# The second feed-forward of an encoder layer by one level of Strassen's algorithm

## Chip, cores and metric

The kernel runs on one core of a Trainium2 chip. The metric is the device time of one execution in microseconds (us). The profile calls the engines PE (TensorE: matmuls; PEld is its weight load), DVE (VectorE), ACT (ScalarE), POOL (GpSimd) and SP (SyncE, which here only issues transfers).

## The reference

One encoder layer on 512 tokens of 1024 channels. Its last part, which the change touches, is a gated feed-forward with 2816 hidden units, behind a norm and a modulation:

```
x = x + g2[:, None, :] * y                       # y: output projection of the token mixing
h = modulate(rms_norm(x, ffn2_norm[l]), sh3, sc3)
x = x + 0.5 * g3[:, None, :] * (silu(h @ w_gate) * (h @ w_up)) @ w_down
return rms_norm(x, final_norm)
```

Before it stand a first feed-forward of the same size, a Fourier branch and an attention branch, and an output projection.

## The kernel before

Activations are held transposed: 128 channels on the partitions, tokens along the free dimension. All data is float32, and every matrix product is made of three: `split` and `split_to` turn a tile into `hi` (a rounded copy, made on ACT, L94 and L107) and `lo` (the residual, a subtraction on DVE, L95 and L108), and `mm3` (L101) runs hi x hi, hi x lo and lo x hi into the same PSUM bank.

The hidden units come in 22 chunks of 128. `ffn` (L244) goes over four parts of 6, 6, 6 and 4 chunks. For each chunk it fetches a unit of `wg` and one of `wu` (each 128 x 1024, 512 KB), splits both, and multiplies them by all 8 chunks of `h`: `products`, 24 matmuls of 512 columns each. `hidden` applies Silu to the gate, multiplies by the up-projection and splits the result. After each part the down projection adds its share to `x` for 8 output chunks. In the second feed-forward the first two chunks (L266 to L274) run in two halves of 256 tokens, so that TensorE can work on the first half while the second is still being normed. The last part's down projection runs in halves too, and `final` norms and stores each half.

Ahead of it, the output projection runs in two parts. The second part (L802 to L821) works by token halves: 8 output chunks into PSUM, added to `x` on DVE (L818), squared on ACT (L229), summed on DVE (L233); then `make_h` makes that half's `h`. In it `inv_rms` (L138) gets the inverse root from two tiny matmuls (L145), a scaling on DVE (L150), a power on POOL (L152), two diagonal tiles on DVE (L157) and a matmul that spreads them (L160). `scaled` (L187) multiplies on DVE into a `t` tile, of which there are two, and `shifted` makes hi on ACT (L194) and lo on DVE (L195).

Tiles come from pools: 5 `raw` tiles for fetched weights, 6 `hi` and 6 `lo` for split ones, 30 general slots of 128 x 1024 (`flex`, by `slot` and `slot32`), two each of the small kinds in `tmp`, 6 PSUM banks for products (`pbank`). A planner orders each engine's instructions when the program is built: it plays the program through with its own costs and gives a free engine the earliest instruction of the text that is ready. On the chip each engine then runs its list in order. Transfers issued by SP wait in SP's queue for a free tile.

## Time and profile before

| | us |
|---|---|
| median of three runs (lowest to highest) | 1095.09 (1093.96 to 1095.14) |
| the profiled execution | 1093.35 |
| its span | 1091.5 |
| TensorE busy in the span | 1067.0 |
| VectorE busy | 607.3 |
| ScalarE busy | 397.5 |

The span reaches from the first to the last instruction that the profiler recorded; the execution's own time is 1.85 us longer. An engine is busy while an instruction runs on it; instructions of one engine overlap a little at their ends, so the distance between starts tells its pace.

### The profile page before, as it was taken

To read this page: it belongs to the slowest core of one execution; us is meant where nothing else is said; L and a number is where in the kernel's file an instruction comes from. 1 tells how busy PE (TensorE), PEld (TensorE's weight loads), DVE (VectorE), ACT (ScalarE), POOL (GpSimd) and SP (SyncE) were. 2 spreads that over 40 slices of the span, in tenths; PEclk is the share of its full clock that TensorE was granted. 3 is DMA by queue.
4 is the path that set the end of the run, shared out by engine and by line. 5 is a ranking of instruction groups with operands and counts; after the bars stand their busy time and mean duration, and the time that the engine had idled before them with its cause. 6 is when DMAs were issued, how large, how long until landed. Compare 5 with 4: busy or idle time off the path is not lost.

```text
span 1091.5 us, 13823 instructions
## 1 busy us (share of the span) xinstructions
PE 1067.0 (98%) x5320; PEld 900.8 (83%) x5320; DVE 607.3 (56%) x1043; ACT 397.5 (36%) x631; POOL 87.0 (8%) x102
## 2 busy tenths in 40 slices
PE   5999999999999999999999989999999999999996
PEld 3888888888888998888888878998888888888886
DVE  6976645862563689752167767784343334334335
ACT  5532222222222444442267664353222222222224
POOL 1000000000000001000155444000000000000000
PEclk9999999999999999999999999999999999999998
DMA  9885642762472156541121223423242233224102
GB/s 360 329 317 166 226 149 87 234 211 76 147 237 99 58 202 218 176 143 39 39 64 54 59 95 108 154 78 107 89 134 82 73 116 116 73 82 135 59 1 78
DMA packets 48643, 143.76 MB, mean 132 GB/s; under 512 B 5489, under 2 KB 9201, under 8 KB 48578
## 3 DMA queue, kind: packets, MB, share of 16 engines
q1 hardware_dynamic: 46738, 137.84, 38.5%
q0 software_dynamic: 1264, 4.52, 1.1%
q8 instruction: 42, 0.69, 0.3%
q10 hardware_dynamic: 576, 0.52, 0.1%
q14 instruction: 23, 0.19, 0.1%
HBM read 138.67 MB, written 4.19 MB: 131 GB/s over the span
## 4 chain that ended last, share of the span: by engine, by line
PE 94%; DVE 2%; ACT 1%; issue 1%; DMA 1%; POOL 1%; SPq 0%; POOLq 0%; DVEq 0%; ACTq 0%
PE ps_mm L102 29%; PE ps_mm L104 29%; PE ps_mm L103 29%; PE ps_mm L324 3%; PE ps_mm L712 1%; PE ps_aux L704 1%; DMA g<-in_xtok 1%; PE ps_aux L160 1%; ACT f L107 0%; PE ps_aux L145 0%; ACT g L692 0%; PE ps_mm L528 0%; PE ps_aux L204 0%; POOL f L108 0%; DVE g L828 0%
## 5 line engine op out<-in xcount | busy, mean ns | idle before, releaser
L103 PE MATMUL ps_mm<-f,hi 128*128 128x512 f32 (+1 forms) x1504 | 550.6, 367 | 0.1
L102 PE MATMUL ps_mm<-f,hi 128*128 128x512 f32 (+1 forms) x1504 | 550.5, 367 | 0.0
L104 PE MATMUL ps_mm<-f,lo 128*128 128x512 f32 (+1 forms) x1504 | 550.1, 366 | 0.0
L94 ACT CAST hi<-raw 128x1024 fp32r<-128x1024 f32 (+4 forms) x207 | 188.3, 913 | 514.5 <-PE ps_mm L103 468.8
L104 PEld LDWEIGHTS ps_mm<-f,lo 128*128 128x128 f32 x1504 | 283.4, 189 | 45.9
L103 PEld LDWEIGHTS ps_mm<-f,hi 128*128 128x128 f32 x1504 | 283.4, 189 | 45.7 <-DVE f L195 0.3
L102 PEld LDWEIGHTS ps_mm<-f,hi 128*128 128x128 f32 x1504 | 283.0, 189 | 45.9 <-ACT f L107 0.6
L95 DVE TENSOR_TENSOR lo<-raw,hi 128x1024 fp32r<-128x1024 f32 (+3 forms) x195 | 213.2, 1095 | 175.5 <-ACT hi L94 171.9
L248 DVE TENSOR_TENSOR sg<-ps_mm,sg 128x512 f32<-128x512 f32 x44 | 30.3, 690 | 128.7 <-PE ps_mm L104 127.9
L133 DVE SCALAR_TENSOR_TENSOR raw<-raw,g 128x1024 f32<-128x1024 f32 x56 | 68.3, 1221 | 33.7 <-DMA raw<-in_ada_w 33.7
L290 DVE SCALAR_TENSOR_TENSOR g<-ps_mm,gate,g 128x512 f32<-128x512 f32 x48 | 35.9, 749 | 56.9 <-PE ps_mm L104 56.9
L152 POOL TENSOR_TENSOR r<-ms,nhalf 128x2 f32<-128x2 f32 x10 | 9.5, 958 | 663.4 <-DVE ms L150 663.4
L107 ACT CAST f<-sg 128x512 fp32r<-128x512 f32 x44 | 27.4, 623 | 18.8 <-DVE sg L248 18.7
L108 DVE TENSOR_TENSOR f<-sg,f 128x512 fp32r<-128x512 f32 x44 | 30.0, 684 | 0.7 <-ACT f L107 0.7
L247 ACT ACTIVATE sg<-ps_mm 128x512 f32<-128x512 f32 x44 | 25.9, 591 | 10.3 <-PE ps_mm L104 9.1
L692 ACT ACTIVATE g<-ps_mm,st 128x512 f32<-128x512 f32 x32 | 22.1, 691 | 19.5 <-DVE st L691 17.2
L324 PE MATMUL ps_mm<-f,hi 128*128 128x512 f32 x96 | 26.5, 414 | 0.7 <-ACT f L210 0.7
L694 POOL TENSOR_SCALAR g<-g,st 128x512 f32<-128x512 f32 x32 | 22.5, 704 | 38.5 <-DVE st L693 31.2
L229 ACT ACTIVATE sq<-g 128x256 f32<-128x256 f32 x42 | 17.0, 413 | 21.1 <-DVE g L308 13.6
L108 DVE TENSOR_TENSOR f<-ps_aux,f 128x512 fp32r<-128x512 f32 x32 | 21.7, 685 | 4.8 <-ACT f L107 4.7
L233 DVE TENSOR_TENSOR ssum<-ssum,sq 128x256 f32<-128x256 f32 x42 | 17.7, 422 | 11.6 <-ACT sq L229 11.4
L133 DVE SCALAR_TENSOR_TENSOR g<-g,g 128x1024 f32<-128x1024 f32 x16 | 19.5, 1219 | 6.8 <-ACT g L351 6.8
(152 smaller groups left out, 723.1 us busy)
## 6 DMA issues: line engine op xcount, KB each, us to landing
raw<-in_ada_w SPq DMA_DIRECT2D x56, 512.0 KB, 4.5
raw<-in_wu SPq DMA_DIRECT2D x45, 512.0 KB, 3.8
raw<-in_wg SPq DMA_DIRECT2D x41, 512.0 KB, 3.5
raw<-in_wd SPq DMA_DIRECT2D x48, 384.0 KB, 3.2
raw<-in_win SPq DMA_DIRECT2D x21, 512.0 KB, 3.5
g<-in_ada_w SPq DMA_DIRECT2D x16, 512.0 KB, 9.3
raw<-in_wd SPq DMA_DIRECT2D x16, 256.0 KB, 2.9
raw<-in_wout SPq DMA_DIRECT2D x16, 256.0 KB, 2.7
```

The costliest lines, as they stand in the source:

```text
L94: nc.scalar.copy(hi[:, :n], raw[:, :n])
L95: engine.tensor_sub(lo[:, :n], raw[:, :n], hi[:, :n].bitcast(F32))
L102: nc.tensor.matmul(out, lhsT=lh, rhs=rh, start=first, stop=False)
L103: nc.tensor.matmul(out, lhsT=lh, rhs=rl, start=False, stop=False)
L104: nc.tensor.matmul(out, lhsT=ll, rhs=rh, start=False, stop=last)
L107: nc.scalar.copy(hi, src)
L108: engine.tensor_sub(lo, src, hi.bitcast(F32))
L133: nc.vector.scalar_tensor_tensor(raw, raw, 1.0, cb.rearrange("p c t -> p (c t)"), op0=ALU.mult, op1=ALU.mult, accum_out=mod[:, j:j + 1])
L247: nc.scalar.activation(sg, pg, AF.Silu)
L248: nc.vector.tensor_mul(sg, pu, sg)
L290: nc.vector.scalar_tensor_tensor(xs(m), out, gate[gk][:, m:m + 1], xs(m), op0=ALU.mult, op1=ALU.add)
L324: nc.tensor.matmul(out[i], lhsT=w[:, i * P:(i + 1) * P], rhs=h1[c][:, part], start=c == 0 and w is wh and part == 0, stop=c == NC - 1 and ...
```

## The change

The gate and up projections of the second feed-forward take two chunks of hidden units at a time (a `Pair`), and multiply them by one level of Strassen's algorithm in Winograd's form. The 1024 x 256 weight matrix is four blocks of 512 x 128, and `h` four blocks of 512 channels x 256 tokens. Seven products of such blocks stand in place of eight, each 4 x 3 matmuls of 256 columns.

On the side of `h`, `make_blocks` makes seven split blocks in place of `h3`: "21" and "11" from the first token half, and from the second "22" and the combinations t1 to t4, each made in place by one operation on 128 x 1024 and then split. On the side of the weights, `_blocks` lays the four blocks out on the host; SP fetches two of them (`first`) and a third (`last`), and the two sums s1 and s3 are made by transfer: SP writes the fourth block twice (`broadcast_to`), and a transfer issued by POOL adds two others onto it (`accum_op`). DVE makes s2 and s4 from these. So a pair has seven splits of 128 x 1024 (`a1` two, `s31` two, `s24` two, `a22` one).

A pair is computed in two steps. `begin` needs only the first token half: two products per matrix into a bank `R1`, whose halves are added to give the first result's tokens. `rest` runs the other five: they accumulate into `R1` and a second bank `R2`, and partial sums are copied out by ACT between products onto the same half of a bank. A first product clears with `start`; the later ones add on (`onto`).

The transfers of the first two pairs (both `first` tiles, and for pair 0 the sums) are issued during the output projection, into general slots; the `begin` of both comes before the `rest` of the first. The down projection takes the last two chunks in reversed order, since a pair finishes its second chunk first.

```diff
-    def mm3(out, lh, ll, rh, rl, first, last):
-        nc.tensor.matmul(out, lhsT=lh, rhs=rh, start=first, stop=False)
-        nc.tensor.matmul(out, lhsT=lh, rhs=rl, start=False, stop=False)
-        nc.tensor.matmul(out, lhsT=ll, rhs=rh, start=False, stop=last)
+    def mm3(out, lh, ll, rh, rl, first, last, onto=False):
+        nc.tensor.matmul(out, lhsT=lh, rhs=rh, start=first, stop=False, skip_group_check=onto)
+        nc.tensor.matmul(out, lhsT=lh, rhs=rl, start=False, stop=False, skip_group_check=onto)
+        nc.tensor.matmul(out, lhsT=ll, rhs=rh, start=False, stop=last, skip_group_check=onto)
...
     def ffn(h, wg, wu, wd, gk, lead, background, after):
+        paired = wg.shape[0] != NF
...
-            elif pi == 0:
-                w = [unit(t[i], D) for i in range(2) for t in (wg, wu)]
-                out = [pbank() for _ in w]
-                for lo, hi in halves:
-                    for i in range(4):
-                        products(f + i // 2, w[i], out[i], lo, hi)
-                for i in range(2):
-                    act.append(hidden(*out[2 * i:2 * i + 2]))
-                f += 2
-            for f in range(f, f0 + nk):
+            elif paired:
+                for i in range(f0 // 2, (f0 + nk) // 2):
+                    pr = ahead[i] if i < len(ahead) else Pair((wg, wu), i)
+                    if i >= len(ahead):
+                        pr.first_weights()
+                    if i == 0:
+                        for p in ahead:
+                            p.first_weights()
+                            p.begin()
+                    pr.weights()
+                    if i >= len(ahead):
+                        pr.begin()
+                    act += pr.rest()
+            for f in range(f, f0 + nk if not paired else 0):
...
+            order = [*range(nk - 2), nk - 1, nk - 2] if paired else [*range(nk)]
...
-                    for k in range(nk):
+                    for k in order:
                         ks = slice(k * P, (k + 1) * P)
-                        mm3(out, dh[:, ks], dl[:, ks], act[k][:, 0], act[k][:, 1], k == 0, k == nk - 1)
+                        mm3(out, dh[:, ks], dl[:, ks], act[k][:, 0], act[k][:, 1], k == 0, k == order[-1])
...
+    class Block:
+        def __init__(self):
+            self.hi, self.lo = (flex.tile([P, 4, HALF], F32R, tag="f", name=nm("b")) for _ in range(2))
+    def make_blocks(lo, hi, ssq, key, sh, half, B, whole):
+        R = inv_rms(ssq.acc, D, hi - lo)
+        def combine(name, src):
+            B[name] = Block()
+            split_to(B[name].hi, B[name].lo, src)
+        def chunk(c):
+            t, _ = scaled(c, lo, hi, R, key)
+            nc.scalar.activation(whole[half][c // 4][:, c % 4], t, AF.Identity, bias=mod_of(sh, c))
+        if half == 0:
+            B["21"], B["11"] = Block(), Block()
+            for k, name in ((1, "21"), (0, "11")):
+                for c in range(4):
+                    chunk(4 * k + c)
+                    split_to(B[name].hi[:, c], B[name].lo[:, c], whole[0][k][:, c])
+            return
+        (h11, h21), (h12, h22) = whole
+        for c in range(4):
+            chunk(c)
+        nc.vector.tensor_sub(h11, h11, h12)
+        combine("t1", h11)
+        for c in range(4, NC):
+            chunk(c)
+        nc.vector.scalar_tensor_tensor(h11, h11, -1.0, h22, op0=ALU.mult, op1=ALU.subtract)
+        combine("t2", h11)
+        nc.vector.tensor_sub(h12, h22, h12)
+        combine("t3", h12)
+        nc.vector.scalar_tensor_tensor(h21, h11, -1.0, h21, op0=ALU.mult, op1=ALU.subtract)
+        combine("t4", h21)
+        combine("22", h22)
+    class Pair:
+        def __init__(self, ws, i, room=None, sums=False):
+            self.ws, self.i, self.sums = ws, i, None
+            room = room or (lambda: wpool.tile([P, SLOT], F32, tag="raw", name=nm("raw")))
+            if sums:
+                self.fetch_sums(room)
+            self.first = []
+            for w in ws:
+                raw = room()
+                nc.sync.dma_start(raw, w[i][:, 0::2])
+                self.first.append(raw)
+            self.E1, self.E2, self.R1, self.R2 = [], [], [], []
+        def fetch_sums(self, room):
+            self.sums = []
+            for w in self.ws:
+                raw = room()
+                nc.sync.dma_start(raw, w[self.i][:, 3:4].broadcast_to([P, 2, S]))
+                nc.gpsimd.dma_start(raw, w[self.i][:, 0:2], accum_op=ALU.add)
+                self.sums.append(raw)
+        def first_weights(self):
+            self.a1 = [split(r, D) for r in self.first]
+        def weights(self):
+            if self.sums is None:
+                self.fetch_sums(lambda: wpool.tile([P, SLOT], F32, tag="raw", name=nm("raw")))
+            last = wpool.tile([P, SLOT], F32, tag="raw", name=nm("raw"))
+            for j, w in enumerate(self.ws):
+                nc.sync.dma_start(last[:, j * S:(j + 1) * S], w[self.i][:, 1])
+            self.s31 = [split(r, D) for r in self.sums]
+            self.s24 = []
+            for r, t in zip(self.first, self.sums):
+                nc.vector.tensor_add(r[:, :S], t[:, S:], r[:, :S])
+                nc.vector.tensor_add(r[:, S:], r[:, :S], r[:, S:])
+                self.s24.append(split(r, D))
+            self.a22 = split(last, D)
+        def product(self, out, w, at, b, first):
+            for c in range(4):
+                cs = slice(at * S + c * P, at * S + (c + 1) * P)
+                mm3(out, w[0][:, cs], w[1][:, cs], h3[b].hi[:, c], h3[b].lo[:, c], first and c == 0, c == 3, not first)
+        def begin(self):
+            for u in range(2):
+                R1 = pbank()
+                self.R1.append(R1)
+                self.product(R1[:, :HALF], self.a1[u], 1, "21", True)
+                self.product(R1[:, HALF:], self.a1[u], 0, "11", True)
+                E1 = tmp.tile([P, S], F32, tag=("sg", "t")[u], name=nm("E1"))
+                self.E1.append(E1)
+                nc.scalar.copy(E1[:, :HALF], R1[:, HALF:])
+                nc.vector.tensor_add(E1[:, :HALF], R1[:, :HALF], E1[:, :HALF])
+            g, up = self.E1
+            nc.scalar.activation(g[:, :HALF], g[:, :HALF], AF.Silu)
+            nc.vector.tensor_mul(g[:, :HALF], up[:, :HALF], g[:, :HALF])
+        def rest(self):
+            for u in range(2):
+                R2 = pbank()
+                self.R2.append(R2)
+                self.product(R2[:, :HALF], self.s31[u], 1, "t1", True)
+                self.product(self.R1[u][:, HALF:], self.s24[u], 0, "t2", False)
+                nc.scalar.copy(self.E1[u][:, HALF:], self.R1[u][:, HALF:])
+            for u in range(2):
+                self.product(self.R1[u][:, HALF:], self.s31[u], 0, "t3", False)
+                E2 = tmp.tile([P, HALF], F32, tag=("sq", "ssum")[u], name=nm("E2"))
+                self.E2.append(E2)
+                nc.scalar.copy(E2, self.R1[u][:, HALF:])
+                nc.vector.tensor_add(E2, self.R2[u][:, :HALF], E2)
+            sg = slot32()[:, 0]
+            for u in range(2):
+                self.product(self.R1[u][:, HALF:], self.a22, u, "t4", False)
+            nc.scalar.activation(sg[:, HALF:], self.E2[0], AF.Silu, scale=-1.0)
+            nc.vector.scalar_tensor_tensor(sg[:, HALF:], self.E2[1], -1.0, sg[:, HALF:], op0=ALU.mult, op1=ALU.mult)
+            nc.scalar.activation(sg[:, :HALF], self.R1[0][:, HALF:], AF.Silu, scale=-1.0)
+            nc.vector.scalar_tensor_tensor(sg[:, :HALF], self.R1[1][:, HALF:], -1.0, sg[:, :HALF], op0=ALU.mult, op1=ALU.mult)
+            second = slot()
+            split_to(second[:, 0], second[:, 1], sg)
+            for u in range(2):
+                self.product(self.R2[u][:, :HALF], self.s24[u], 1, "22", False)
+                E1 = self.E1[u][:, HALF:]
+                nc.vector.tensor_add(E1, self.R2[u][:, :HALF], E1)
+                if u == 0:
+                    nc.scalar.activation(E1, E1, AF.Silu)
+            g, up = self.E1
+            nc.vector.tensor_mul(g[:, HALF:], up[:, HALF:], g[:, HALF:])
+            s = slot()
+            split_to(s[:, 0], s[:, 1], g)
+            return [s, second]
...
+    def room():
+        return slot32().rearrange("p h t -> p (h t)")
+    h3 = {}
+    ahead = [Pair((a["wg2"], a["wu2"]), i, room, not i) for i in range(2)]
     units = []
     for m in range(0, NC, 2):
         raw = wpool.tile([P, SLOT], F32, tag="raw", name=nm("raw"))
         for j in range(2):
             nc.sync.dma_start(raw[:, j * 4 * P:(j + 1) * 4 * P], a["wout"][m + j, :, 4:8, :])
         units.append(split(raw, SLOT))
-    h3 = [slot() for _ in range(NC)]
+    whole = [[flex.tile([P, 4, HALF], F32, tag="f", name=nm("w")) for _ in range(2)] for _ in range(2)]
...
-        make_h(h3, lo, hi, ssq, "3", SH3)
+        make_blocks(lo, hi, ssq, "3", SH3, lo // HALF, h3, whole)
...
-    ffn(h3, a["wg2"], a["wu2"], a["wd2"], "3", None, lambda: None, final)
+    ffn(None, a["wg2"], a["wu2"], a["wd2"], "3", None, lambda: None, final)
...
+def _blocks(w):
+    u = _units(w).reshape(NF // 2, 2, P, 2, S)
+    return np.ascontiguousarray(np.stack([u[:, 0, :, 0], u[:, 1, :, 1], u[:, 0, :, 1], u[:, 1, :, 0]], axis=2))
...
-        "wg2": _units(v["ffn2_w_gate"][0]), "wu2": _units(v["ffn2_w_up"][0]), "wd2": _units(v["ffn2_w_down"][0]),
+        "wg2": _blocks(v["ffn2_w_gate"][0]), "wu2": _blocks(v["ffn2_w_up"][0]), "wd2": _units(v["ffn2_w_down"][0]),
```

## Rows read from the trace of the kernel before

**Rows 1.** The page: busy time of the engines, and the chain that ended last, by engine.
```profile
PE 1067.0 (98%) x5320; PEld 900.8 (83%) x5320; DVE 607.3 (56%) x1043; ACT 397.5 (36%) x631; POOL 87.0 (8%) x102
...
PE 94%; DVE 2%; ACT 1%; issue 1%; DMA 1%; POOL 1%; SPq 0%; POOLq 0%; DVEq 0%; ACTq 0%
```

**Rows 2.** Windows at the hand-over: busy time by engine, clock, DMA share, GB/s.
```profile
684.00:707.00 23.00, 23.00 (x160) 21.26 (x158) 17.11 (x30) 7.63 (x14) 0.71 (x1) 1.00 0.48 159
707.00:719.00 12.00, 11.85 (x98) 11.79 (x98) 11.08 (x29) 9.34 (x18) 0.00 (x0) 1.00 0.00 1
719.00:731.00 12.00, 11.98 (x98) 11.66 (x97) 10.85 (x23) 3.15 (x7) 1.61 (x1) 1.00 0.51 177
731.00:742.50 11.50, 11.50 (x91) 11.16 (x90) 7.99 (x12) 8.31 (x11) 0.00 (x0) 1.00 0.33 89
```

**Rows 3.** Timeline of PE, matmuls of 512 and of 256 columns: start, duration.
```profile
684.98 0.39 PE L102 MATMUL ps_mm<-f,hi 128*128 128x512 f32 x1
...
691.55 0.39 PE L104 MATMUL ps_mm<-f,lo 128*128 128x512 f32 x1
691.77 0.28 PE L102 MATMUL ps_mm<-f,hi 128*128 128x256 f32 x1
...
694.89 0.28 PE L104 MATMUL ps_mm<-f,lo 128*128 128x256 f32 x1
```

**Rows 4.** Timeline of DVE, 719 to 726.
```profile
719.36 1.22 DVE L95 TENSOR_TENSOR lo<-raw,hi 128x1024 fp32r<-128x1024 f32 x1
720.50 0.42 DVE L233 TENSOR_TENSOR ssum<-ssum,sq 128x256 f32<-128x256 f32 x1
720.83 1.22 DVE L95 TENSOR_TENSOR lo<-raw,hi 128x1024 fp32r<-128x1024 f32 x1
...
725.38 0.86 DVE L189 SCALAR_TENSOR_TENSOR t<-g,G,ps_aux 128x256 f32<-128x256 f32 x2
```

**Rows 5.** Timeline of ACT: first and last of four casts, and three in succession.
```profile
706.94 1.05 ACT L94 CAST hi<-raw 128x1024 fp32r<-128x1024 f32 x1 [1.08 <-PE ps_mm L103]
...
716.41 1.05 ACT L94 CAST hi<-raw 128x1024 fp32r<-128x1024 f32 x1 [0.71 <-PE ps_mm L103]
...
736.48 1.04 ACT L94 CAST hi<-raw 128x1024 fp32r<-128x1024 f32 x1
737.42 0.62 ACT L107 CAST f<-sg 128x512 fp32r<-128x512 f32 x1
737.94 1.06 ACT L94 CAST hi<-raw 128x1024 fp32r<-128x1024 f32 x1
```

**Rows 6.** Groups by line and shape, 690 to the end: busy us, mean ns.
```profile
L95 DVE TENSOR_TENSOR lo<-raw,hi 128x1024 fp32r<-128x1024 f32 x48 | 58.7, 1224 | 43.8 <-ACT hi L94 41.2
...
L94 ACT CAST hi<-raw 128x1024 fp32r<-128x1024 f32 x48 | 50.6, 1053 | 141.8 <-PE ps_mm L103 130.1 <-issue 11.7
...
L229 ACT ACTIVATE sq<-g 128x256 f32<-128x256 f32 x28 | 11.4, 414 | 14.8 <-DVE g L818 7.4 <-DVE g L308 7.3
...
L189 DVE SCALAR_TENSOR_TENSOR t<-g,G,ps_aux 128x256 f32<-128x256 f32 x16 | 7.1, 474 | 0.4 <-PE ps_aux L160 0.4
```

**Rows 7.** DMA issues of the whole run: KB each, median us to landing.
```profile
raw<-in_wu SPq DMA_DIRECT2D x45, 512.0 KB, 3.8
...
x_kept<-g POOLq DMA_DIRECT2D x4, 512.0 KB, 2.9
...
g<-x_kept POOLq DMA_DIRECT2D x4, 512.0 KB, 5.3
```

**Rows 8.** Timeline of POOL: issuing four transfers, and two powers of the norms.
```profile
647.36 2.20 POOL L778 DMA_DIRECT2D g<-x_kept  x4
...
705.88 0.71 POOL L152 TENSOR_TENSOR r<-ms,nhalf 128x2 f32<-128x2 f32 x1 [27.34 <-DVE ms L150]
722.20 1.61 POOL L152 TENSOR_TENSOR r<-ms,nhalf 128x2 f32<-128x2 f32 x1 [15.61 <-DVE ms L150]
```

More of the change, by code (lines that the diff above doesn't have):

```diff
@@ L303, in ffn @@
                         out = pbank()
-                        for k in range(nk):
+                        for k in order:
                             ks = slice(((m % 2) * nk + k) * P, ((m % 2) * nk + k + 1) * P)
                             mm3(out[:, :hi - lo], dh[:, ks], dl[:, ks], act[k][:, 0, lo:hi], act[k][:, 1, lo:hi],
-                                k == 0, k == nk - 1)
+                                k == 0, k == order[-1])
                         nc.vector.scalar_tensor_tensor(xs(m, lo, hi), out[:, :hi - lo], gate[gk][:, m:m + 1],
```

## The prediction

> **What bounds the kernel now.** I read the page first: TensorE is busy for 1067.0 of the 1091.5 us span, and the chain that ended last is 94% TensorE [rows 1]. So time is won only by giving TensorE less to do, and lost wherever something makes it wait. Next I read the windows around the place of the change, the hand-over from the output projection to the second feed-forward [rows 2]. TensorE is busy 11.85 of 12, 11.98 of 12 and 11.50 of 11.5 us there. VectorE beside it is busy 11.08 of 12 and 10.85 of 12, and only then 7.99 of 11.5. The reader is to see two full engines: TensorE hides everything today, but VectorE has about 2 us to spare in 24. Then I read the starts of the matmuls [rows 3], not their durations, which overlap (0.28 and 0.39 us). With 256 columns there are 26 steps from 691.77 to 694.89, so 0.120 us a matmul; with 512 columns 29 steps from 684.98 to 691.55, so 0.2266 us. Half the columns cost 53%, not 50%.
>
> **TensorE's work.** Before, the first two chunks of hidden units run in two token halves: 4 weight units x 8 x 3 x 2 = 192 matmuls of 256 columns, 192 x 0.120 = 23.0 us. The other 20 chunks run 20 x 2 x 8 x 3 = 960 matmuls of 512 columns, 960 x 0.2266 = 217.5 us. Together 240.5 us. After, each of 11 pairs has two weight matrices x 7 products x 4 chunks x 3 = 168 matmuls of 256 columns: 1848 x 0.120 = 221.8 us. Saved: 18.7 us. A product of Strassen's algorithm is 12 matmuls, 1.44 us; a pair is 20.2 us.
>
> By the Trainium skill (TensorE: Matmul & The Clock Gate, "Back-to-back issue gap") a warm matmul costs its columns over 2.4 GHz plus 2.5 ns, so an estimate of 109 ns for 256 columns and 216 ns for 512. By that the work would fall from 228.2 to 201.8 us, 26.4 us saved. The rows have 120 and 227 ns, and they decide.
>
> **VectorE and ScalarE in a pair.** Back-to-back starts are closer than durations. On VectorE a 1024-wide subtraction takes 1.14 us (719.36 to 720.50) and a 256-wide operation 0.33 (720.50 to 720.83); a scaled one of 256 takes 0.39 (two in 0.86, the second lasting 0.47) [rows 4, 6]. For 512 I interpolate between 0.33 and 1.14: 0.60. On ScalarE a 1024-wide copy takes 0.94 and a 512-wide one 0.52 [rows 5]; a 256-wide one lasts 0.41 [rows 6]. The operations on the hidden values are priced by their rows of the same width, though the changed kernel's read PSUM more often.
>
> A pair has 7 splits (8.0 us on VectorE, 6.6 on ScalarE), 4 block sums of 512 (2.4 on VectorE), ten copies and Silus of 256 on ScalarE (4.1) with two 512-wide copies (1.0), and on VectorE 3 operations of 256 at the begin (1.0), then five of 256 (1.7), two scaled ones (0.8) and two of 512 (1.2). VectorE: 15.1 of 20.2 us; ScalarE: 11.7 of 20.2. Two chunks of before cost VectorE four splits and four operations of 512: 7.0 of 21.8 us. So VectorE's load doubles to 75%. It still fits, if it isn't late.
>
> **Where the start costs.** Before, TensorE fills the wait for the second norm with the first half's products. After, it has only the two `begin`s there. The output projection's second part starts at 691.77 [rows 3] and takes 192 x 0.120 = 23.0 us; with some 1.2 us of norm matmuls it ends near 716.0. Four `begin` units are 11.5 us, the second half's norm matmuls 1.2, so at 728.7 TensorE wants t1. The first scaled chunk of the second half starts at 725.38 [rows 4]. Four chunks take until about 727.9, the subtraction 1.2, the copy on ScalarE 1.05, the residual 1.2, with hand-overs: t1 is there at 731.6. So TensorE waits at least 2.9 us.
>
> The rest is a matter of VectorE's throughput. It is full from 707 on [rows 2]. Up to the last thing that TensorE needs for pair 1's first four products, VectorE does: first-half blocks 8 x 0.72 = 5.8; second-half evictions and squares 5.8; norms 1.0; the second pair's two opening splits and the first pair's five others 8.0; two `begin`s 2.0; eight scaled chunks 3.1; four block combinations and five block splits of 1024 10.3; the first pair's `rest` 3.7; pair 1's four splits 4.6 and four sums 2.4. That is 46.7 us, so 753.7 without a gap. TensorE would want it at 728.7 + 14.4 + 4.3 = 747.4. That is 6.3 us late, and VectorE will stand still for some 2 us behind the chain of t1 and t2. I take 8.5 us. The lower bound is 2.9 (the chain alone, with the other work pulled ahead into free time before 707), the upper 12 (6.3 plus the chain's 2.9, and 2.8 for ScalarE, which has 9.34 of 12 us filled at 707 to 719 and gets eight more copies of 256 there, 3.3 us).
>
> The weights' splits wait for tiles as before: the four casts from 706.94 to 716.41 [rows 5] follow the release of a `hi` tile each, and the new ones stand in the same places. The two early pairs' six transfers go out during the output projection into free slots; I cost them at nothing, because SP's 512 KB land in 3.8 us [rows 7] and there are over 20 us to spare; without that cover pair 0 would start some 9 us later.
>
> **Later pairs.** In a pair the same PSUM half is read between products. Three times only one product, 1.44 us, lies between the last matmul and the next onto the same bank. Of that 0.16 is the matmul's tail (0.28 less 0.12) and 0.41 the read; 0.87 us are left. If ScalarE has just begun a 1.05 us copy, TensorE waits some 0.2 to 0.3 us. Bounds: nothing, and 33 x 0.27 = 9 us. ScalarE's splits fill a third of the time, so I take 2 us, nearest to none.
>
> The sums are new: SP writes a block twice, then POOL's queue adds two blocks from memory onto it. An adding transfer is nowhere in the trace. The nearest rows are POOL's plain ones, 512 KB landing in 2.9 and 5.3 us [rows 7]; issuing four takes POOL 2.2 us [rows 8]. The two tiles come free about 2 us into a pair, when the sums are used; 3.8 + 0.6 + 5.3 lands near 12, and the next pair's sums are needed, split, at 25.9. Some 8 to 11 us are spare with the split queue allowed for, so I take nothing; doubling 5.3 would still be hidden. Bytes rise from 2.1 to 3.7 MB a pair, 182 GB/s; 177 GB/s took a DMA share of 0.51 [rows 2]. Behind a waiting addition on POOL stands only the power for the norm, which the second half's blocks wait for: 0 to 3.8 us, at 0 if it is issued before 720, as free tiles allow.
>
> POOL's small power takes 0.71 us beside an idle VectorE and 1.61 beside a busy one [rows 8]: 0.9 us more. The Trainium skill (SBUF — State Buffer, "SBUF: two separate sides") says that VectorE and GpSimd lock a shared port pair against each other, and that some VectorE operations keep GpSimd from writing the descriptors of its own transfers. By the row's 0.9 an addition is hidden still, and the sum unchanged; a longer lock-out is the second rival below.
>
> The down projections read the same data; the last chunk now comes second last. Its closing chain of about 2 us is under five k-steps, 5 x 3 x 0.2266 = 3.4 us, as now: nothing, or 1 us in each of four parts without that cover. The flag on the matmuls, the weights' new order in memory and the smaller tiles cost nothing on an engine.
>
> **Sum.** 18.7 - 8.5 - 2 = 8.2 us gained on the profiled 1093.35 us (span 1091.5): 1085.2. That execution lies 1.74 under the median of the runs, 1095.09, so I forecast 1087 us.
>
> **Rivals.** First, the start is nearly free: the planner pulls the sums and splits ahead of 707, and only the chain's 2.9 us stays. 18.7 - 2.9 - 0 = 15.8: 1079. For it speaks that VectorE is busy only 17.11 of the 23 us before 707 [rows 2]; against it that `hi` and `lo` tiles come free only from 706.94 on.
>
> Second, the additions decide: if an addition takes longer than about 13 us, every pair without a down projection just before it waits; these are 7 of 11. It becomes a loss when each waits over 1.2 us, at an addition of some 15 us. At four times 5.3, 21 us, it is 7 x 8 = 56 us: 1143. For it speaks that POOL is slower beside VectorE, which is 75% busy now, and that an addition also reads its target; against it 8 us of slack.
>
> Third, the short hand-overs: all 33 waits at 0.27 and a start of 12 us take 21 and leave nothing: 1097, at the edge of no change. That TensorE saves less than counted can hardly be: both pitches stand in the rows.
>
> **Chances.** Forecast 0.56 (its own range 1083 to 1092), free start 0.16, hand-overs eat it 0.15, additions late 0.13. A measurement here can tell about 0.2%, 2.2 us, so faster is below 1092.9: 0.72, from the first two cases; within 0.2%: 0.13; slower: 0.15, the additions and a little of the third. The range goes from the free start, 1079, to 1098 just past the third rival.
>
> **What would show it.** Right: TensorE with 1848 matmuls of 256 columns at 0.120 in this stage; a gap of some 3 us near 729 before the t1 products, released by VectorE, and some 8 us in all up to 757; then windows with over 98% TensorE and VectorE near 75%. Wrong: TensorE waiting on sums in each pair, behind ScalarE's casts of them, with adding transfers landing after 13 us or more; or ScalarE's 256-wide copies as releaser 33 times.

## The result, and the profile after

| | us |
|---|---|
| before, median of 6 runs | 1094.91 (1093.93 to 1095.65) |
| after, median of 6 runs | 1103.18 (1099.59 to 1104.64) |
| ratio, 95% interval | 1.0071 (1.0053 to 1.0089) |
| the profiled execution, and its span | 1104.14, 1102.3 |

The change made the kernel 8 us slower. The forecast was 1087, and the time lies beyond the range. The six runs after spread over 5 us, and the profiled one lies 1 us above their median. The page of the kernel after, its busy times and its closing chain, against [rows 1]:

```profile
PE 1061.8 (96%) x6016; PEld 928.6 (84%) x6016; DVE 703.8 (64%) x1209; ACT 461.4 (42%) x765; POOL 106.2 (10%) x124
...
PE 81%; DVE 6%; issue 4%; DMA 3%; ACT 3%; POOL 2%; SPq 0%; POOLq 0%; DVEq 0%; ACTq 0%
```

TensorE's share of the chain fell from 94% to 81%: the other 19% are other engines, transfers and issuing. The windows of the hand-over, with the stretch behind them (columns as in [rows 2]):

```profile
684.00:707.00 23.00, 19.46 (x114) 17.48 (x113) 12.19 (x16) 4.62 (x6) 2.59 (x3) 0.93 0.94 280
707.00:719.00 12.00, 7.55 (x51) 7.35 (x50) 7.22 (x19) 3.12 (x9) 0.71 (x1) 0.82 0.32 63
719.00:731.00 12.00, 12.00 (x90) 11.82 (x90) 11.34 (x29) 11.78 (x27) 0.00 (x0) 0.89 0.01 2
731.00:742.50 11.50, 11.04 (x89) 10.58 (x87) 9.39 (x18) 7.53 (x14) 1.61 (x1) 1.00 0.01 1
742.50:757.00 14.50, 9.01 (x42) 8.12 (x43) 14.50 (x18) 8.65 (x13) 0.00 (x0) 0.72 0.10 36
```

Two holes are to be seen. The first, from 696 to 719, stands where TensorE was full before, and there VectorE too is idle: 7.22 of 12 us where it had 11.08. In the second, 742.5 to 757, VectorE is full. The first was not in the forecast. In both the granted clock falls, to 1.2 GHz for 20.5 us in all between 701 and 760.

How it adds up. The first eviction of the first down projection comes at 807.09, before it came at 788.46: 18.6 us later, though TensorE has 6.1 us less to do up to there (23.0 + 192 x 0.2266 against 504 x 0.120). So the start lost 24.7 us, not the 8.5 of the forecast. The next two parts took 66.85 us each in place of 69.36, 2.5 saved of 4.8, and the last 43.78 in place of 46.25, 2.5 of 3.2: the later pairs lost 5.3 us, not 2. 18.8 less 30.0 is 11.2 more; the down projections, 0.2 shorter each, and the end bring it to the 10.8 between the two profiled executions.

What TensorE waited for between 690 and 757, by the view of the waits (us in total, times, longest):

```profile
PE ps_aux L146 <- DVE ssum L234: 4.5, 1, 4.5
PE ps_mm L103 <- DVE g L947: 3.2, 1, 3.2
PE ps_mm L104 <- DVE b L109: 3.0, 2, 1.9
PE ps_mm L103 <- ACT b L108: 2.0, 1, 2.0
```

The first two make the first hole: an eviction of the output projection (L947), and the sum of squares for the first norm (L234). The last two are the second hole, the split blocks of the second half. With three shorter rows of the view the waits come to 14.0 us. The 20.5 us at half clock cost up to 10 more, an estimate (half of them). Together that is 24, close to the 24.7 that the start lost. SP's list shows where the first comes from (start, time to issue):

```profile
670.51 4.52 SPq L957 DMA_DIRECT2D raw<-in_wout  x4
675.08 0.42 SPq L384 DMA_DIRECT2D g<-in_wg  x1
...
679.53 1.70 SPq L376 DMA_DIRECT2D g<-in_wu  x1
681.33 4.10 SPq L957 DMA_DIRECT2D raw<-in_wout  x4
```

The six early transfers stand between the two halves of the weights of the projection's second part, 3 MB ahead of four pieces that are wanted first. POOL issues pair 0's two additions beside them, at 681.64 and 685.63, another 1 MB. From issue to landing the four pieces took (the view of L957, 681 to 686):

```profile
DMA to landing us min/median/max: 13.0/14.5/14.8
```

ScalarE stood idle for 14.25 us until the first two of them had landed:

```profile
696.93 1.04 ACT L94 CAST hi<-raw 128x1024 fp32r<-128x1024 f32 x1 [14.25 <-DMA raw<-in_wout]
```

And VectorE, whose list goes on in order, stood with it:

```profile
698.00 1.23 DVE L95 TENSOR_TENSOR lo<-raw,hi 128x1024 fp32r<-128x1024 f32 x1 [10.78 <-ACT hi L94]
699.15 0.74 DVE L947 SCALAR_TENSOR_TENSOR g<-ps_mm,mod,g 128x512 f32<-128x512 f32 x1
699.81 1.22 DVE L95 TENSOR_TENSOR lo<-raw,hi 128x1024 fp32r<-128x1024 f32 x1
700.94 0.75 DVE L947 SCALAR_TENSOR_TENSOR g<-ps_mm,mod,g 128x512 f32<-128x512 f32 x1
701.60 1.22 DVE L95 TENSOR_TENSOR lo<-g,hi 128x1024 fp32r<-128x1024 f32 x1
702.85 0.69 DVE L400 TENSOR_TENSOR g<-g,g 128x512 f32<-128x512 f32 x1
703.46 0.75 DVE L947 SCALAR_TENSOR_TENSOR g<-ps_mm,mod,g 128x512 f32<-128x512 f32 x1
```

Evictions (L947) stand behind residuals (L95), the residuals behind casts, the casts behind transfers. From 701.60 on splits and sums of the early pairs, which TensorE wants only after 719, stand between the evictions too. The transfers of these 30 us, and over the whole run those issued by POOL (KB each, median us to landing):

```profile
raw<-in_wout SPq DMA_DIRECT2D x8, 256.0 KB, 8.6
g<-in_wg SPq DMA_DIRECT2D x3, 512.0 KB, 10.8
g<-in_wu SPq DMA_DIRECT2D x3, 512.0 KB, 11.8
...
raw<-in_wg POOLq DMA_DIRECT2D x10, 512.0 KB, 7.3
raw<-in_wu POOLq DMA_DIRECT2D x10, 512.0 KB, 7.0
```

Each number is a median. The 8.6 mixes the four pieces ahead of the early transfers (2.5 to 4.1 us) with the four behind them, and of the early six the five with a recorded landing took 6.0 to 16.0 us. In the same 30 us of the kernel before:

```profile
raw<-in_wout SPq DMA_DIRECT2D x8, 256.0 KB, 2.9
```

### The profile page after: what moved, and what is told of

It reads as the page before. It is cut to its first block, busy times and chain, and to the rows that moved or that the text cites. A ratio compares the mean times of both kernels' runs of the same rounds, so it can differ in the third digit from the quotient of the medians.

```text
span 1102.3 us, 15667 instructions
## 1 busy us (share of the span) xinstructions
PE 1061.8 (96%) x6016; PEld 928.6 (84%) x6016; DVE 703.8 (64%) x1209; ACT 461.4 (42%) x765; POOL 106.2 (10%) x124
## 4 chain that ended last, share of the span: by engine, by line
PE 81%; DVE 6%; issue 4%; DMA 3%; ACT 3%; POOL 2%; SPq 0%; POOLq 0%; DVEq 0%; ACTq 0%
PE ps_mm L103 25%; PE ps_mm L104 25%; PE ps_mm L105 24%; PE ps_mm L470 3%; DMA raw<-in_wg 1%; DMA raw<-in_wout 1%; DVE lo L95 1%; PE ps_mm L858 1%; PE ps_aux L850 1%; ACT hi L94 1%; ACT f L108 1%; POOL yb L935 1%; DMA g<-in_xtok 1%; DVE f L109 1%; PE ps_aux L161 1%
## 5 line engine op out<-in xcount | busy, mean ns | idle before, releaser
L103 PE MATMUL ps_mm<-f,hi 128*128 128x512 f32 (+1 forms) x1120 | 409.9, 368 | 3.6 <-DVE g L947 3.2
L104 PE MATMUL ps_mm<-f,hi 128*128 128x512 f32 (+1 forms) x1120 | 410.0, 367 | 0.0
L105 PE MATMUL ps_mm<-f,lo 128*128 128x512 f32 (+1 forms) x1120 | 409.0, 366 | 0.0
L94 ACT CAST hi<-raw 128x1024 fp32r<-128x1024 f32 (+4 forms) x230 | 211.5, 925 | 394.8 <-PE ps_mm L104 340.9
L95 DVE TENSOR_TENSOR lo<-raw,hi 128x1024 fp32r<-128x1024 f32 (+3 forms) x218 | 240.8, 1108 | 150.7 <-ACT hi L94 148.4
L103 PEld LDWEIGHTS ps_mm<-f,hi 128*128 128x128 f32 x1120 | 212.3, 190 | 37.5 <-DVE g L947 3.4
L104 PEld LDWEIGHTS ps_mm<-f,hi 128*128 128x128 f32 x1120 | 212.8, 190 | 34.3 <-DVE f L109 1.0
L105 PEld LDWEIGHTS ps_mm<-f,lo 128*128 128x128 f32 x1120 | 212.7, 190 | 33.1
L103 PE MATMUL ps_mm<-b,hi 128*128 128x256 f32 x616 | 177.7, 289 | 4.4 <-ACT b L108 2.0
L104 PE MATMUL ps_mm<-b,hi 128*128 128x256 f32 x616 | 176.4, 286 | 3.0 <-DVE b L109 3.0
L105 PE MATMUL ps_mm<-b,lo 128*128 128x256 f32 x616 | 176.0, 286 | 0.0
L103 PEld LDWEIGHTS ps_mm<-b,hi 128*128 128x128 f32 x616 | 119.5, 194 | 6.9 <-ACT b L108 2.4
L104 PEld LDWEIGHTS ps_mm<-b,hi 128*128 128x128 f32 x616 | 119.9, 195 | 3.6 <-DVE b L109 3.4
L105 PEld LDWEIGHTS ps_mm<-b,lo 128*128 128x128 f32 x616 | 119.9, 195 | 0.0
L400 DVE TENSOR_TENSOR raw<-raw,raw 128x512 f32<-128x512 f32 x18 | 12.4, 689 | 22.2 <-DMA raw<-in_wg 19.5
```

Of the source, the lines that this page charges most:

```text
L94: nc.scalar.copy(hi[:, :n], raw[:, :n])
L95: engine.tensor_sub(lo[:, :n], raw[:, :n], hi[:, :n].bitcast(F32))
L103: nc.tensor.matmul(out, lhsT=lh, rhs=rh, start=first, stop=False, skip_group_check=onto)
L104: nc.tensor.matmul(out, lhsT=lh, rhs=rl, start=False, stop=False, skip_group_check=onto)
L105: nc.tensor.matmul(out, lhsT=ll, rhs=rh, start=False, stop=last, skip_group_check=onto)
L400: nc.vector.tensor_add(r[:, :S], t[:, S:], r[:, :S])
```

## The experiments

The experiments ran on two chips, and the kernel before had medians from 1094.38 to 1094.5 beside them. All times are medians, and differences are between medians.

**The projection's weights first.** SP issues all of `wout` and then the early transfers.

```diff
-    ahead = [Pair((a["wg2"], a["wu2"]), i, room, not i) for i in range(2)]
     units = []
...
-            nc.sync.dma_start(raw[:, j * 4 * P:(j + 1) * 4 * P], a["wout"][m + j, :, 4:8, :])
+            fetched = nc.sync.dma_start(raw[:, j * 4 * P:(j + 1) * 4 * P], a["wout"][m + j, :, 4:8, :])
         units.append(split(raw, SLOT))
+    with tc.issue_after(fetched.ins):
+        ahead = [Pair((a["wg2"], a["wu2"]), i, room, not i) for i in range(2)]
```

> Theory A, the early transfers delay the output projection's own weights: with the weights of its second part issued ahead of the six pair transfers, TensorE's waits of 3.4 and 4.6 us before 716 and the half clock that follows them go, some 11 of the 13 us lost before 722; about 1092 us. Rival B, the added work on VectorE or the planned order makes those waits: nothing changes, about 1103 us.

Measured: 1099.28 (1098.72 to 1100.98), ratio 1.0046 (1.0031 to 1.0061), 3.9 us less than the change, where theory A promised 11. Two of the change's six runs lie in this range, so the size is uncertain by some 2 us; the same order costs 3.3 in a cleaner pair of kernels below. The wait of 3.2 for L947 is gone, that of 4.7 for L234 stays. VectorE's list says why:

```profile
689.87 0.74 DVE L947 SCALAR_TENSOR_TENSOR g<-ps_mm,mod,g 128x512 f32<-128x512 f32 x1
694.35 1.23 DVE L95 TENSOR_TENSOR lo<-g,hi 128x1024 fp32r<-128x1024 f32 x1 [3.74 <-ACT hi L94]
697.51 0.69 DVE L400 TENSOR_TENSOR g<-g,g 128x512 f32<-128x512 f32 x1 [1.94 <-DMA g<-in_wg]
698.12 0.74 DVE L947 SCALAR_TENSOR_TENSOR g<-ps_mm,mod,g 128x512 f32<-128x512 f32 x1
```

A residual of an early block and the sum behind an addition (L400) wait for their transfers, and the eviction waits behind them, 8 us after the one before it.

**Without the combined blocks.** As above, with t1 to t4 and their splits gone.

```diff
-        nc.vector.tensor_sub(h11, h11, h12)
-        combine("t1", h11)
...
-        combine("t4", h21)
         combine("22", h22)
+        B["t1"] = B["t3"] = B["11"]
+        B["t2"] = B["t4"] = B["21"]
```

> As e1_wout_first, and the combinations t1 to t4 and their splits are left out (other blocks stand in their place, so that part of the computation is wrong): 8 VectorE operations of 1.14 us and 4 ScalarE copies fewer. If VectorE's blocks are what TensorE waits for between 742 and 756, the 6.4 us of waits and the half clock behind them go, some 10 us under e1_wout_first. If it is the weights' splits that are late, e1_wout_first's time stays within 2 us.

Measured, in one run: 1089.71, 9.6 us below the kernel with `wout` first. TensorE is full from 742.5 to 757 (14.50 of 14.5 us at full clock), and the wait of 4.7 us at 707 stays. So the second hole is the work on the blocks, the first is not. ScalarE's four copies of the blocks are gone too, but in the change it was VectorE that was full there (14.50 of 14.5 us, ScalarE 8.65).

**TensorE kept busy.** Two groups of idle matmuls, 42 in all, ahead of the places where it waits for the blocks.

```diff
+                    if i == 0:
+                        keep_busy(24)
                     pr.weights()
...
+                if self.i == 0 and u == 0:
+                    keep_busy(18)
                 self.product(self.R1[u][:, HALF:], self.s24[u], 0, "t2", False)
```

> As e1_wout_first, with 24 idle matmuls of 256 columns (2.9 us) before the first rest and 18 (2.2 us) behind its first product, which nothing reads. If the half clock after the waits costs time of its own, TensorE stays at full clock and some 4 us are won against e1_wout_first. If TensorE only waits for VectorE there, whatever its clock, the time is that of e1_wout_first within 1 us.

Measured: 1098.51 (1097.15 to 1099.12), 0.8 us less than without them, and the ranges overlap; by the two intervals the difference is uncertain by some 2 us. The clock stood at 1.2 GHz for 3.4 us there in place of 10.2. So no cost of the clock's own is shown in this place, which fits a TensorE that would wait for VectorE at either level. What the half clock behind the first hole costs by itself was not tried.

**The early pairs' work behind the evictions.** With `wout` first; the early splits, sums and `begin`s are queued on ScalarE and VectorE behind the first half's last square and sum.

```diff
-                        for p in ahead:
-                            p.first_weights()
-                            p.begin()
-                    pr.weights()
+                        with tc.issue_after(half_done[0].ins), tc.issue_after(half_done[1].ins):
+                            for p in ahead:
+                                p.first_weights()
+                                p.begin()
+                            pr.weights()
+                    else:
+                        pr.weights()
```

> As e1_wout_first, with all VectorE and ScalarE work of the first two pairs' weights queued behind the first half's squares. If VectorE's list holds the output projection's evictions behind residuals and sums whose transfers are late, TensorE's wait of 4.9 us at 710 and its half clock go; that work then falls into VectorE's full stretch after 707, which gives part of it back: 1092 to 1096 us, against e1_wout_first's 1099. If something else makes the wait at 710, it stays and the time is 1099 us or more.

Measured: 1093.35 in 10 runs (1091.61 to 1095.59), ratio 0.9994 (0.9984 to 1.0003): 5.9 us less than with `wout` first, and level with the kernel before. The wait for L234 is gone, and one for t1's cast takes its place:

```profile
PE ps_mm L103 <- ACT b L108: 5.0, 1, 5.0
PE ps_mm L104 <- DVE b L109: 1.9, 2, 1.3
PE ps_aux L161 <- DVE dg L158: 1.7, 1, 1.7
```

The stall came from the order of the list. What is pushed back is missing at 731, where VectorE is full (11.50 of 11.5 us up to 742.5), but the gain comes back: by the matmuls in the windows this kernel is 50 ahead of the one with `wout` first at 719, 19 at 742.5, and 50 again at 757. At 0.120 us these are 6.0 us, the 5.9 measured.

**The first pair by eight products.** With `wout` first, the first two chunks run in token halves as before, from blocks "11", "21", "12" and "22", and Strassen's algorithm begins with the second pair. TensorE does 24 matmuls more, 2.9 us.

```diff
-        ahead = [Pair((a["wg2"], a["wu2"]), i, room, not i) for i in range(2)]
+        plain = []
+        for part in (slice(0, None, 2), slice(1, None, 2)):
+            for w in (a["wg2"], a["wu2"]):
+                raw = room()
+                nc.sync.dma_start(raw, w[0][:, part])
+                plain.append(raw)
+        ahead = [None, Pair((a["wg2"], a["wu2"]), 1, room)]
...
+                    for half, names in ((0, ("11", "21")), (1, ("12", "22"))):
+                        for j in range(4):
+                            for k in range(2):
```

> As e1_wout_first, but the first pair of chunks runs by eight products in two token halves as before the change, and Strassen's form starts with the second pair. TensorE has 24 matmuls or 2.9 us more to do, but 17.3 us of work, not 11.5, that needs the first token half alone, and five splits and four sums fewer. If the hand-over is bound by VectorE and the chain to t1, about 1092 - 12 + 3 = 1083 us. If the later pairs are late anyway, about 1092 us.

Measured: 1084.58 (1084.06 to 1086.22), ratio 0.9911 (0.9895 to 0.9928). Both holes are closed, and the clock stays full (same columns):

```profile
696.00:707.00 11.00, 10.87 (x89) 10.46 (x88) 6.65 (x18) 3.14 (x8) 2.51 (x3) 1.00 0.90 245
707.00:719.00 12.00, 11.98 (x98) 11.94 (x99) 11.54 (x29) 11.61 (x27) 0.00 (x0) 1.00 0.01 2
...
742.50:757.00 14.50, 13.70 (x112) 13.23 (x111) 12.87 (x15) 7.41 (x12) 1.76 (x2) 1.00 0.67 143
```

The eight products of the second half need two split blocks and no combination, so TensorE has 11.5 us of work (8 x 1.44) while VectorE makes t1 to t4. This edit also spares VectorE five splits and four sums, and the queue pair 0's two additions; which of these closes which hole was not separated.

**The same with the transfers in the change's place.** The early transfers go back between the two halves of `wout`.

> As e6_plain_first, but with the six early transfers issued where the change issues them, ahead of the last half of the projection's weights; no additions are among them. If the order in SP's queue alone makes the first wait, 3 to 4 us and some half clock come back: 1088 to 1091 us. If it was the additions beside them that made the weights late, it stays near 1085 us.

Measured: 1087.9 (1087.19 to 1090.7), 3.3 us more, and no run reaches down to the range of the one before; TensorE waits 2.1 us for L234 at 705.8. SP's order costs about the same here as in the change, 3.9, though no addition is among the early transfers. The four pieces of `wout` behind them landed in 8.1 to 8.9 us here, in the change in 13.0 to 14.8, so the additions and the transfers under them may have lengthened the wait there.

**Each addition twice.** The kernel with a plain first pair, and POOL's addition repeated.

```diff
                 nc.gpsimd.dma_start(raw, w[self.i][:, 0:2], accum_op=ALU.add)
+                nc.gpsimd.dma_start(raw, w[self.i][:, 0:2], accum_op=ALU.add)
```

> As e6_plain_first, but each block sum is added twice by transfer, one after the other (so the sums are wrong). The prediction held the later pairs' additions hidden up to about 13 us: then the time stays within 3 us of 1085. If the additions, which land in 7 us beside VectorE's waiting list, already stand at the edge, each of the seven pairs without a down projection ahead waits 5 us or more: 1115 us or more.

Measured: 1150.57 (1148.7 to 1151.98), 66 us more than with one addition, for transfers that landed in 5.8 to 6.2 us. ScalarE's and VectorE's lists in one pair of it:

```profile
880.33 0.37 ACT L451 COPY E<-ps_mm 128x256 f32<-128x256 f32 x1
886.94 1.04 ACT L94 CAST hi<-raw 128x1024 fp32r<-128x1024 f32 x1 [6.24 <-DMA raw<-in_wg]
887.89 0.37 ACT L451 COPY E<-ps_mm 128x256 f32<-128x256 f32 x1
```

```profile
886.86 0.69 DVE L415 TENSOR_TENSOR raw<-raw,raw 128x512 f32<-128x512 f32 x1 [12.96 <-DMA raw<-in_wg]
887.47 1.22 DVE L95 TENSOR_TENSOR lo<-raw,hi 128x1024 fp32r<-128x1024 f32 x1
888.61 0.75 DVE L452 TENSOR_TENSOR E<-ps_mm,E 128x256 f32<-128x256 f32 x2
```

The cast and the sums of the next pair (L94, L415) wait for their addition, and behind them stand this pair's own copy and partial sum (L451, L452), which TensorE needs at once. It waited 33.8 us for such copies, 6 times, and 12.5 for the sums of `begin`; the clock at half for 47.8 us took up to another 24, an estimate. It did not wait for the additions themselves. The two sums of this pair had landed at 886.84 and 889.33, and TensorE came to its first products with them at 900.24 and 903.12. In the other pairs the distance is 11 us or more too. But TensorE was late itself by then: unstalled, 20.2 us after 866.58, where it began the five products of the pair before, it would have come at 886.8, about when they landed. So whether other lists would hide a doubled addition is not shown.

**`begin` ahead of `weights`.** The plain first pair; in the text, a pair's first products come before its other weights.

```diff
-                    pr.weights()
                     if i >= len(ahead):
                         pr.begin()
+                    pr.weights()
```

> As e6_plain_first, with a later pair's begin ahead of its weights in the text, so that VectorE's list prefers the first results to the sums. If the remaining waits of 0.9 and 1.2 us at the pairs' starts come from that order, 2 to 4 us are won: 1081 to 1083 us. If not, within 1 us of 1085.

Measured: 1083.10 (1082.83 to 1083.91), ratio 0.9894 (0.9879 to 0.9909), the best here, 1.5 us under the plain first pair, and below every run of that one, which ran on the other chip. With single additions the same place of VectorE's list reads:

```profile
850.38 0.69 DVE L414 TENSOR_TENSOR raw<-raw,raw 128x512 f32<-128x512 f32 x1 [5.97 <-DMA raw<-in_wg]
851.10 0.69 DVE L415 TENSOR_TENSOR raw<-raw 128x512 f32<-128x512 f32 x1
851.71 1.22 DVE L95 TENSOR_TENSOR lo<-raw,hi 128x1024 fp32r<-128x1024 f32 x1
852.85 0.42 DVE L451 TENSOR_TENSOR E<-ps_mm,E 128x256 f32<-128x256 f32 x1
```

VectorE waits 5.97 us for the addition here as well, and this pair's partial sum (L451) stands behind it. It ends at 853.27, and TensorE's product onto that bank was due at 853.2: just in time.

**The later sums in general slots**, on the kernel with `begin` first, with one addition and with two. Until then the suspicion was that the five `raw` tiles, in which everything goes round, start the additions late.

```diff
             if self.sums is None:
-                self.fetch_sums(lambda: wpool.tile([P, SLOT], F32, tag="raw", name=nm("raw")))
+                self.fetch_sums(room)
```

> The version with begin ahead of weights, and the sums of every later pair fetched into general slots, which are free earlier, and not into the five raw tiles that all weights go round in. Theory A: the ring of five raw tiles sets when an addition starts, so the slack is used up before it begins; with own slots the last short waits (0.4 to 0.9 us, under 3 us in all) go and the time is 1081 to 1083 against 1083.1. Theory B: the addition's own 7 us and POOL's one-after-another issue set it; no change, 1083 +- 1.

> The same with each addition transferred twice, so the sums are wrong by one block. Doubling cost 66 us where the sums went round in the raw tiles. Theory A (ring of raw tiles): with own slots the doubled additions start far earlier and are hidden; within 10 us of the kernel with single additions, below 1093. Theory B (the additions themselves are too slow): 30 us or more over it, above 1113.

Measured: 1124.01 (1123.06 to 1124.9) and 1126.56 (1126.33 to 1130.53), ratios 1.0268 (1.0251 to 1.0285) and 1.0302 (1.0283 to 1.032). Both theories missed the first kernel by 40 us. TensorE's waits in it from 740 on:

```profile
PE ps_mm L105 <- DVE lo L95: 13.3, 7, 1.9
PE ps_mm L103 <- ACT hi L94: 11.1, 8, 2.5
```

With other tiles the planner wrote another list, as ScalarE's shows:

```profile
775.12 0.37 ACT L433 COPY E<-ps_mm 128x256 f32<-128x256 f32 x1 [1.59 <-PE ps_mm L105]
775.39 1.99 ACT L94 CAST hi<-g 128x1024 fp32r<-128x1024 f32 x2
```

The casts of the sums now stand behind the copies of the pair's own `begin`, at the moment when TensorE wants them; the two sums had landed at 772.37 and 775.21. So seven pairs wait 3.3 to 4.2 us for them, 24.4 in all, and 1.8 for copies; 30.7 us at half clock take some 15 more, an estimate: the 41 us. With the sums' work that late, the second addition costs 2.5 us, not 66. In three pairs it then lands only 1.2 us before TensorE's product, so there the addition has begun to count itself. All this fits a price that follows from where the readers stand in the lists. The two kernels differ from the earlier ones in the tiles and in POOL's order as well (the two additions of a pair go out 1.3 us apart, not 4), so this pair alone doesn't prove it; the rows of the doubled additions show the mechanism.

## Why the prediction was wrong, step by step

**TensorE's work: right.** All 1848 matmuls of 256 columns are there (3 lines of 616), 0.120 us apart wherever nothing is late. The best version has 1872 of them, 224.6 us by that step, 15.9 less than before, and 11.4 of these reached the time. The formula that the Trainium skill (TensorE: Matmul & The Clock Gate, "Back-to-back issue gap") gives for an isolated warm matmul would make them 109 ns, an estimate; starts in the kernel after are 120 ns apart, as before, and the measurement decides.

**Early transfers at nothing: the step that failed first.** The prediction said "I cost them at nothing, because SP's 512 KB land in 3.8 us and there are over 20 us to spare". The spare time was there, since TensorE wants these blocks only at 719. But the price was not theirs: they landed in 6.0 to 16.0 us, the pieces of `wout` behind them in 13.0 to 14.8 in place of 2.9, and their readers in VectorE's list held up evictions. SP's order measured 3.9 us (3.3 with a plain first pair), the order of the lists 5.9, both with half clock in them. With the 3.3 us by which the later pairs lost more than the forecast's 2, that is 13 of the 16 us by which the forecast missed; the rest is not assigned. The DMA share of 0.48 in the 23 us before 707 [rows 2], into which SP's 3 MB and POOL's 1 MB were put, looks like room. It is a mean over a full stretch and an empty one of the kernel before (columns as there):

```profile
684.00:696.00 12.00, 12.00 (x72) 10.64 (x71) 10.44 (x14) 4.65 (x6) 0.00 (x0) 1.00 0.85 275
696.00:707.00 11.00, 11.00 (x91) 10.62 (x89) 6.67 (x17) 2.99 (x8) 0.71 (x1) 1.00 0.09 34
```

**The start, +8.5: mechanism right, size right for its own part, in part by luck.** The waits for blocks at 742 to 756 are 5.0 us, the first of them 2.0 before t1 (2.9 in the forecast), and without t1 to t4 the kernel is 9.6 us faster; 8.5 lies between. The list of VectorE's work ended near 754 in the forecast, and VectorE is full until 757. But from 707 on it was busy for 42.5 of the 50 us (7.22, 11.34, 9.39 and 14.50), where the forecast had 46.7 without a gap: some of the list was done before 707, and VectorE stood idle in the first hole. The first hole itself was not in the sum. That such a sum can be avoided shows in the plain first pair: 2.9 us more of TensorE's work, 14.7 us less time.

**The clock: not in the forecast.** Half clock after the waits took up to 10 us of TensorE's time between 701 and 760 (20.5 us at half pace, an estimate). In the second hole, where VectorE sets the pace, mending 6.8 us of it won 0.8 us, within the noise. With the sums in slots, 26.2 us of waits alone don't make up the 41 us; with half of the 30.7 us at half clock added they do.

**Additions with 8 to 11 us of slack: the cost of nothing held, by luck.** They land in 7.0 to 7.3 us (medians), between the row of 5.3 and the 13 that the prediction allowed, so the second rival did not come. Up to TensorE's need the slack was there: in the kernel with `begin` first the later pairs' sums landed some 11 us or more ahead of their first products. But "doubling 5.3 would still be hidden" is refuted: 66 us. The prediction took TensorE's need, 25.9 us into a pair, as the due time. The lists read the sums 11.5 us earlier, ahead of copies and partial sums of the pair in work: at 850.38 in the pair shown, whose `rest` began at 841.7, so that TensorE wants them a pair later, at 861.9. The true slack in that place is none: the product onto the partial sum's bank comes eight products after 841.7, at 853.2, and the partial sum ended at 853.27.

**Later pairs, +2: 5.3.** It lay within the bounds, 0 to 9. Of the 2.3 us in each part of three pairs, 1.3 stand as two waits (steps between starts, less 0.12): 0.41 for a copy that ScalarE had behind the cast of the next pair's sum, itself waiting 0.63 for its addition, and 0.87 for a sum of `begin` that VectorE had behind two residuals (2.36). The rest is in pieces below 0.3 us and was not traced. With a plain first pair, `begin` ahead of `weights` won 1.5 us.

**POOL's power at 0: right.** The two powers took 0.71 and 1.61 us, as in [rows 8], and VectorE waited 1.4 us for them in all, before and after. That row again fits the lock between VectorE and GpSimd that the Trainium skill describes (SBUF — State Buffer, "SBUF: two separate sides"). An addition took POOL 0.86 us to issue, and no run shows a longer lock-out.

**Open:** whether lists that read the sums between their landing and TensorE's need would hide the doubled addition at the full gain, and how much of the first hole is due to pair 0's additions rather than to the plain transfers. Neither was tried.

## What to carry to other kernels

On engines that run their lists in order, a transfer's slack ends where its first reader stands in a list, not where the matmul needs the data: price an early fetch by what is queued behind it on the DMA queue and behind its readers. When an algorithm saves TensorE's work by additions on another engine, count that engine's load where it is already full, here the 40 us after the first norm. Doing that one place the old way turned a loss of 8 us into a gain of 6.6 (1087.9), and with `wout` first and `begin` ahead of `weights` into 11.4. And a planner that writes lists from its own costs can turn a small change of tiles into 40 us, so compare the order of the lists before the times.

## What the runs showed of the hardware

A transfer that adds onto its target landed in 7.0 to 7.3 us for 512 KB, where plain ones of this kernel took 3.7 to 4.3, and two in a row onto one tile 5.8 to 6.2 each (all medians). Six transfers of 512 KB issued within 6 us, with two additions beside them, landed in 6.0 to 16.0 us, and four pieces of 256 KB behind them in 13.0 to 14.8, at 280 GB/s and a DMA share of 0.94. TensorE's granted clock fell to half (1.2 GHz) after a wait of 3.2 us in the change, in or after one of 4.7 with `wout` first, and in the second of two of 2.0 and 1.1 us close together, but not after a lone one of 2.1 (the plain first pair in the change's order).
